# A tile of its own for a head's turned squares and spread root, in the second pass of a matrix memory

## The chip, the cores and the metric

The kernel runs on one core of one Trainium2 chip. The metric is device time in microseconds (us), taken as the median of several runs. Beside it stands one profiled execution, which tells when each instruction ran and what it waited for. The engines are named as in the profile: PE is the matmul engine (PEld its weight loads), DVE the vector engine, ACT the scalar engine, POOL the GpSimd engine, SP the engine that issues most DMAs.

## The reference

One encoder layer is applied to two inputs of 512 tokens by 1024 channels, `x_prompt` and `x_sample`, with the same weights: a half-step SwiGLU FFN, a mixing block, a second half-step FFN, a last RMSNorm. The mixing block runs grouped-query attention and an mLSTM matrix memory with 4 heads of 128 channels side by side. The change touches the end of the memory, where each head's output is normed over its 128 channels and gated:

```python
h = (h_fwd + h_bwd).transpose(0, 2, 1, 3)
h = h * lax.rsqrt(jnp.mean(h * h, axis=-1, keepdims=True) + EPS)
h = h.reshape(B, S, M_WIDTH) * head_norm.astype(jnp.float32)
return (jax.nn.sigmoid(o_pre.astype(jnp.float32)) * h).astype(q.dtype)
```

## The kernel before

All products are done in float32 split into a high and a low part (three matmuls for one product), on 128x512 tiles with channels on the partitions and the 512 tokens along the row. The mixing block is the generator `mix(s, ...)`, which runs once for each input; `s = 0` is the prompt, `s = 1` the sample. A scheduler orders the instructions of each engine by priority, and pools hand out tiles: a pool's tag has a fixed number of tiles, and a new tile of that tag starts when an older one's last user is done. Two tags matter here, both of 128x512 float32 tiles: `f2` with four tiles and `R` with two (`T2` at the top of the kernel hands them out, `F2()` in `mix` is `T2` with tag `f2`).

In the second pass (`s = 1`) the memory of a head goes through four steps, and the heads are interleaved with other products by the list at the end of `mix`'s memory part:

- `mem_head(h)` (L1291 and below) makes the weights of the head, four tiles of 128 tokens by 512. Its products on PE are L1302.
- `mem_blocks` turns them by DVE in 32x32 pieces into two tiles `qt` (L1340), and `mem_send` (L1348) lets POOL issue eight DMAs that write them to a DRAM buffer `tbuf`.
- `mem_out(h, ...)` fetches them back, turned as a whole: for each of the four blocks POOL issues a DMA into a tile `p = F2()` (L1361). In the profile this is `f<-tbuf`. Each block is split in two: ACT makes the upper half (L727) and DVE the lower half (L728, which also reads `p`, and so frees it). PE multiplies them with the values `Vm` (L1374, three matmuls for a block, twelve for a head). The marked instructions of this step keep their place in the program.
- Then the head is normed. ACT copies the result out of PSUM (L1380) and squares it (L1383). DVE turns the squares into `turned_` (L225, in `block_sums`), sums them to a small `row` (L226); PE folds `row` (L232); DVE makes the reciprocal root by small operations (L235 to L241), spreads it over `turned_` (L258, in `spread_rows`), and multiplies (L1391). ACT and DVE split the product into `mem` (L727, L728). The steps from L232 on carry a later priority, so they stand in the order behind work of the next head.

So `turned_` is written at L225, read at L226, written again at L258 and read last at L1391. It lives for about a head's time, while the next head's four blocks are being fetched into tiles of the same tag.

Beside this PE works through units of 24 or 12 matmuls (L850) that need no part of the memory: gates, and the projection of the attention (`merge_att`, `mg<-mg,mm` at L1269 on DVE). Their weights were split in the first pass and are loaded again by SP (L293, `w<-wpark`, two DMAs of 512 KB for a unit), into four tiles that come free when PE has finished a unit. SP also loads `w_out` (L271) into tiles that the sent `qt` tiles free. Near the end of the pass, `prep2` loads a tile of the first input from `x2buf` (L1808) into an `f2` tile, norms it on DVE (L723) and stores it to `xnbuf` (L1810). The `R` tiles hold rows that are spread over all partitions (`R2[0]`, which `prep2` reads) and running sums of squares.

Of the kernel before, what the change touches and what calls it, by code (L numbers as in the profile page):

```python
# [8 lines left out]
F32 = mybir.dt.float32  # L9
# [17 lines left out]
def encoder(ctx, tc, I, outs):  # L27
# [14 lines left out]
    def nm(s):  # L42
        n_id[0] += 1
        return f"{s}_{n_id[0]}"

    @contextmanager
    def shifted(n):

        tc.cur_priority += n
        yield  # L50
        tc.cur_priority -= n
# [8 lines left out]
    def T2(dtype=F32, tag="t2"):  # L60
        if tag in ("eb", "ac"):
            i = boxes[tag]
            boxes[tag] += 1
            return boxes["tile"][:, i % 4 + (4 if tag == "ac" else 0), :]
        if tag == "R":
            return spool.tile([P, S], dtype, tag="R", bufs=2, name=nm("R"))
        n = {"t2": 11, "f2": 4}[tag]
        return tpool.tile([P, S], dtype, tag=tag, bufs=n, name=nm(tag))
# [41 lines left out]
    def PO():  # L110
        return po_.tile([P, S], F32, tag="o", name=nm("pso"))
# [4 lines left out]
    def PT():  # L116
        return pt.tile([P, S], F32, tag="t", name=nm("pst"))
# [16 lines left out]
    def A(shape, dtype=F32, name="a"):  # L134
        return apool.tile(shape, dtype, tag="a", name=nm(name))
# [85 lines left out]
    def block_sums(t, q=None):  # L221

        row = spool.tile([P, 64], F32, tag="row", bufs=1, name=nm("row"))
        q = T2(F32, "f2") if q is None else q
        nc.vector.transpose(q, t)  # L225
        nc.vector.tensor_reduce(row[:, 0:16], q.rearrange("p (n j) -> p n j", j=32), axis=AX.X, op=ALU.add)  # L226
        return row

    def block_rstd(row, n, keep=lambda i: i):

        p = PT()
        keep(nc.tensor.matmul(p[:, 0:16], fold, row[:, 0:16], start=True, stop=True))  # L232
        V = nc.vector
        a, y, u = [row[:, 16 * i:16 * i + 16] for i in (1, 2, 3)]
        V.tensor_scalar(a, p[:, 0:16], 1.0 / n, EPS, op0=ALU.mult, op1=ALU.add)  # L235
        V.tensor_scalar(u.bitcast(I32), a.bitcast(I32), 1, None, op0=ALU.logical_shift_right)
        V.tensor_scalar(y.bitcast(I32), u.bitcast(I32), -1.0, 1597463007.0, op0=ALU.mult, op1=ALU.add)
        for _ in range(3):
            V.scalar_tensor_tensor(u, y, -0.5, y, op0=ALU.mult, op1=ALU.mult)
            V.tensor_tensor(u, u, a, op=ALU.mult)  # L240
            V.scalar_tensor_tensor(y, u, 1.5, y, op0=ALU.add, op1=ALU.mult)  # L241
        return y
# [13 lines left out]
    def spread_rows(r16, R):  # L256

        nc.vector.transpose(R.rearrange("p (n j) -> p n j", j=32), r16.unsqueeze(2).to_broadcast([P, 16, 32]))  # L258
        return R
# [465 lines left out]
    def split(src, hi, lo, eng=None):  # L725

        nc.scalar.activation(hi, src, AF.Copy)  # L727
        (eng or V_).tensor_tensor(lo, src, f(hi), op=ALU.subtract)  # L728
# [54 lines left out]
    def mark(i, last):  # L783
        return pin(i) if last and marks[0] else i
# [74 lines left out]
    def mix(s, xh, xl, early=None, extra=None, after=None):  # L859
# [9 lines left out]
        def F2(dtype=F32):  # L869
            return T2(dtype, "f2")  # L870
# [417 lines left out]
            return up_unit(1, d, mem, done, (PS, PT)[d % 2])  # L1288

        mem = A([P, HM, 2, S], F32R, "mem")  # L1290

        def mem_head(h):
            qk = qks[h]
# [58 lines left out]
        def mem_out(h, Ts):  # L1352
            moved = isinstance(Ts, int)
            vm = Vm[0]
            po = PO()
            hs_ = slice(h * P, (h + 1) * P)
            turned = []
            for j in range(4 + 1):
                if j < 4 and moved:
                    p = F2()  # L1360
                    mark(nc.gpsimd.dma_start(p, tbuf[Ts][4 * j:4 * j + 4].rearrange("c r a x -> (c r) (a x)")), True)  # L1361
                elif j < 4:
                    p = PT()
                    for i in range(4):
                        nc.tensor.transpose(p[:, i * P:(i + 1) * P], Ts[i][0][:, j * P:(j + 1) * P], ident)
                if j < 4:
                    ph, pl = T2(F32R), T2(F32R)
                    split(p, ph, pl)
                    turned.append((j, ph, pl))
                if j >= 1:  # L1370
                    t, ph, pl = turned.pop(0)
                    with shifted(15):
                        for n, (a, b) in enumerate(((0, ph), (1, ph), (0, pl))):
                            mark(nc.tensor.matmul(po, vm[:, a, t, hs_], b, start=(t == 0 and n == 0),  # L1374
                                                  stop=(t == 3 and n == 2)), True)
            h2 = T2()
            og = ogs[h]
            if moved:
                rows_ = T2()
                nc.scalar.activation(rows_.rearrange("p (i a m) -> p i a m", i=4, a=4),  # L1380
                                     po.rearrange("p (a i m) -> p i a m", i=4, a=4), AF.Copy)
                po = rows_
            nc.scalar.activation(h2, po, AF.Square)  # L1383
            V_.scalar_tensor_tensor(og, og, 1.0, po, op0=ALU.add, op1=ALU.mult)
            turned_ = F2()
            row = block_sums(h2, turned_)
            with shifted(60):
                rh = block_rstd(row, DM)
            with shifted(160):
                Rh = spread_rows(rh, turned_)  # L1390
                V_.scalar_tensor_tensor(og, og, hn[:, h:h + 1], Rh, op0=ALU.mult, op1=ALU.mult)  # L1391
                split(og, mem[:, h, 0, :], mem[:, h, 1, :])

        if s:
            qk2, qk3 = [[mem_qk(h, j) for j in range(2)] for h in (2, 3)]
            ma = [merge_att(d) for d in range(KD)]
            marks[0] = True
            q = mem_blocks(0, mem_head(0))
            at = [mem_send(*q)]
            go(*mem_values(), *qk2)  # L1400
            q = mem_blocks(1, mem_head(1))
            go(*qk3, ma[0], ma[1])
            mem_out(0, at[0])
            at.append(mem_send(*q))
            q = mem_blocks(2, mem_head(2))
            go(att_gate(6), att_gate(7), ma[2], ma[3])
            mem_out(1, at[1])
            at.append(mem_send(*q))
            q = mem_blocks(3, mem_head(3))
            go(*ma[4:])  # L1410
            mem_out(2, at[2])
            at.append(mem_send(*q))
            go(*[mem_gate(d) for d in range(EARLY)])
            mem_out(3, at[3])
            marks[0] = False
# [354 lines left out]
    R = [None, None]  # L1770
# [14 lines left out]
    def mid_parts(s):  # L1785
# [10 lines left out]
        return one, two, three  # L1796

    m0 = mix(0, *nhl[0], None, mid_parts(1), prep1)
    for _ in range(3):
        next(m0)  # L1800
# [27 lines left out]

    R2 = [None, None]
    m1 = mix(1, *nhl[1], None, parts2(0), prep2)  # L1830
    next(m1)
    next(m0)
# [150 lines left out]
```

## Time and profile before

| what | value |
|---|---|
| time, median of 3 runs | 2033.63 us (2033.22 to 2034.94) |
| profiled execution: time | 2034.22 us |
| profiled execution: span of the core | 2032.4 us |
| mean granted clock of PE over the span | 0.998 |
| busy: PE, DVE, ACT, POOL | 2016.1, 1593.8, 919.9, 253.4 us |
| second pass of the memory, from its first L1302 on PE to the start of its last L1391 | 1168.3 to 1311.9 us of the span |

The span runs from the first to the last instruction of the core; the time is longer by what lies around it. A row of the timeline gives start, length, engine, line and operation, the tiles written and read, how many instructions are merged in the row, and in brackets how long the engine stood idle before it and what released it. "Granted clock" is the share of PE's full clock that the chip allowed. Waits are inferred from semaphores: an instruction that waits for several is put down to the last of them.

### The profile page before, as it was taken

The numbers are of one execution on the slowest core, as the hardware profiler recorded it, in microseconds if no ns is written. First come the engines' busy times: TensorE is split into PE (matmuls) and PEld (weight loads), VectorE is DVE, ScalarE is ACT, GpSimd is POOL, SyncE is SP. The second block draws the span as 40 slices with busy tenths as digits, with TensorE's granted clock in tenths as the row PEclk, the third lists the DMA queues.
The fourth block names the chain that finished last, engine by engine and source line by source line (L and its number), as shares of the span: only waits on it lengthen the run. The fifth ranks groups of instructions, "written<-read, shape, count | busy, mean of one in ns | idle before, by whom it ended". The sixth has DMA issues, their size and how long they took to land.

```text
span 2032.4 us, 26876 instructions
## 1 busy us (share of the span) xinstructions
PE 2016.1 (99%) x9129; PEld 1662.1 (82%) x9129; DVE 1593.8 (78%) x2830; ACT 919.9 (45%) x1677; POOL 253.4 (12%) x313
## 2 busy tenths in 40 slices
PE   9999999999999999999999999999999999999998
PEld 7888888888888887888888877888888888888887
DVE  7989999996698787886567867367798988786797
ACT  7644444443224477663325754145444444442224
POOL 0233333301003000100120022011000000000001
PEclk9999999999999999999999999999999999999999
DMA  9778786899766765868556677767565655699753
GB/s 312 232 234 266 237 276 229 276 346 363 270 218 225 266 195 184 282 212 293 194 188 209 195 246 259 252 204 242 159 208 169 227 166 180 204 334 348 270 199 120
DMA packets 329546, 482.11 MB, mean 237 GB/s; under 512 B 23016, under 2 KB 196160, under 8 KB 328128
## 3 DMA queue, kind: packets, MB, share of 16 engines
q1 hardware_dynamic: 316352, 439.27, 64.9%
q0 software_dynamic: 12896, 40.86, 5.8%
q8 instruction: 72, 1.18, 0.2%
q14 instruction: 66, 0.54, 0.1%
q10 hardware_dynamic: 160, 0.27, 0.0%
HBM read 308.70 MB, written 171.61 MB: 236 GB/s over the span
## 4 chain that ended last, share of the span: by engine, by line
PE 94%; DVE 2%; DMA 2%; ACT 1%; issue 0%; SPq 0%; DVEq 0%; ACTq 0%; POOLq 0%
PE mm L850 15%; PE pso L374 12%; PE pst L374 11%; PE mm L374 10%; PE mm L644 9%; PE pss L374 6%; PE mm L836 4%; PE pss L644 4%; PE pst L644 4%; PE mm L815 3%; PE pso L644 3%; PE pss L1112 1%; PE pso L1159 1%; PE pst L850 1%; PE pss L850 1%; PE pss L1302 1%
## 5 line engine op out<-in xcount | busy, mean ns | idle before, releaser
L374 PE MATMUL pst<-xc,w 128*128 128x512 f32 x1056 | 253.8, 389 | 1.0 <-ACT t L409 1.0
L374 PEld LDWEIGHTS pst<-xc,w 128*128 128x128 f32 x1056 | 198.2, 188 | 42.5 <-ACT t L409 1.4
L374 PE MATMUL mm<-xc,w 128*128 128x512 f32 x972 | 229.7, 390 | 0.3 <-ACT f L382 0.3
L374 PEld LDWEIGHTS mm<-xc,w 128*128 128x128 f32 x972 | 181.9, 188 | 38.6 <-ACT f L382 0.8
L644 PE MATMUL mm<-rt,w 128*128 128x512 f32 x765 | 178.7, 389 | 0.0
L850 PE MATMUL mm<-xh,w 128*128 128x512 f32 x560 | 176.3, 392 | 0.0
L644 PEld LDWEIGHTS mm<-rt,w 128*128 128x128 f32 x765 | 143.5, 188 | 29.7
L332 ACT ACTIVATE w<-t 128x512 fp32r<-128x512 f32 x176 | 107.5, 628 | 132.2 <-issue 63.1
L333 DVE TENSOR_TENSOR w<-t,w 128x512 fp32r<-128x512 f32 x176 | 120.8, 704 | 30.6 <-ACT w L332 28.9
L374 PE MATMUL pso<-xc,f 128*128 128x512 f32 x528 | 127.2, 390 | 0.1
L374 PE MATMUL pss<-xc,w 128*128 128x512 f32 x528 | 126.8, 389 | 0.0
L374 PE MATMUL pso<-xc,w 128*128 128x512 f32 x528 | 126.8, 389 | 0.0
L850 PEld LDWEIGHTS mm<-xh,w 128*128 128x128 f32 x560 | 105.2, 188 | 22.0
L374 PEld LDWEIGHTS pso<-xc,f 128*128 128x128 f32 x528 | 98.9, 188 | 21.5 <-DVE t L413 1.0
L374 PEld LDWEIGHTS pss<-xc,w 128*128 128x128 f32 x528 | 99.1, 188 | 20.6
L374 PEld LDWEIGHTS pso<-xc,w 128*128 128x128 f32 x528 | 99.1, 188 | 20.6
L836 PE MATMUL mm<-xh,w 128*128 128x512 f32 x336 | 110.4, 395 | 0.0
L850 PE MATMUL mm<-xl,w 128*128 128x512 f32 x280 | 109.7, 392 | 0.0
L727 ACT ACTIVATE w<-wr 128x512 fp32r<-128x512 f32 x72 | 45.1, 632 | 138.4 <-PE pso L644 70.6
L727 ACT ACTIVATE w<-t 128x512 fp32r<-128x512 f32 x82 | 51.8, 632 | 107.4 <-PE pst L644 62.4
L644 PE MATMUL pss<-rt,w 128*128 128x512 f32 x396 | 93.7, 389 | 0.0
L644 PE MATMUL pst<-rt,w 128*128 128x512 f32 x396 | 93.7, 389 | 0.0
(461 smaller groups left out, 4169.6 us busy)
## 6 DMA issues: line engine op xcount, KB each, us to landing
rt<-rbuf SPq DMA_DIRECT2D x154, 512.0 KB, 5.7
w<-wpark SPq DMA_DIRECT2D x112, 512.0 KB, 5.0
wpark<-w SPq DMA_DIRECT2D x64, 512.0 KB, 3.9
wr<-in_ffn_w_gate_dram SPq DMA_DIRECT2D x62, 512.0 KB, 5.5
wr<-in_ffn_w_up_dram SPq DMA_DIRECT2D x44, 512.0 KB, 4.7
rbuf<-f SPq DMA_DIRECT2D x86, 256.0 KB, 4.5
rbuf<-R SPq DMA_DIRECT2D x82, 256.0 KB, 4.7
rbuf<-tab SPq DMA_DIRECT2D x74, 256.0 KB, 4.1
```

What stands on the lines that cost most here:

```text
L332: pin(nc.scalar.activation(t[:, 0], src, AF.Copy))
L333: pin(V_.tensor_tensor(t[:, 1], src, f(t[:, 0]), op=ALU.subtract))
L374: nc.tensor.matmul(p, a[:, k, :], xt[:, b, k, :], start=(first and k == 0 and i == 0), stop=(k == HK_ - 1 and i == 2), skip_group_check=True)
L644: nc.tensor.matmul(p, u[:, a, d * P:(d + 1) * P], r[:, b, ts], start=(first and q == 0 and k == 0), stop=(q == len(us) - 1 and k == 2), sk ...
L727: nc.scalar.activation(hi, src, AF.Copy)
L815: mark(nc.tensor.matmul(p[b][:, :N], a[:, k, bs], w_[:, kl, :], start=(k == 0 and i == 0), stop=(k == KD - 1 and i == 2)), (kl, b, i) == ( ...
L836: pin(nc.tensor.matmul(p[0], a[:, k, :], b, start=(k == 0 and i == 0), stop=(k == n - 1 and i == 2)))
L850: mark(nc.tensor.matmul(p, a[:, k, :], b, start=(k == 0 and i == 0), stop=last), last)
L1112: pin(nc.tensor.matmul(p, qT[:, h, b * P:(b + 1) * P], kv[:, hk * 2 + j, :], start=(j == 0), stop=(j == 1)))
L1159: pin(nc.tensor.matmul(pos[h], Vst[:, kb, h // 4, :], w, start=(kb == KBS[0] and i == 0), stop=(kb == KBS[3] and i == 1)))
L1302: nc.tensor.matmul(p, qk[a][:, isl], qk[b], start=(n == 0), stop=(n == 2))
```

## The change

```diff
@@ in mix(), after merge_mem, before mem_head
         mem = A([P, HM, 2, S], F32R, "mem")
+        own = [T2(F32, "R")] if s else []
 
@@ in mem_out()
             nc.scalar.activation(h2, po, AF.Square)
             V_.scalar_tensor_tensor(og, og, 1.0, po, op0=ALU.add, op1=ALU.mult)
-            turned_ = F2()
+            turned_ = own[0] if own else F2()
             row = block_sums(h2, turned_)
```

In the second pass, one tile of tag `R` is taken once, and all four heads use it as `turned_`. In the first pass nothing changes. No instruction is added or removed; lines behind the first edit move down by one (L1361 becomes L1362, L1374 becomes L1375, and so on). What moves is decided by the scheduler and the pools, and shows in the order at three places.

POOL, the fetches of head 2's four blocks and the sends of head 3, with the semaphores that each waits for (`DMASW` are POOL's own DMAs); before:

```order
L1361 DMA f_1450_11386<-tbuf_259 128x512 [waits DMASW2_49,DMASW1_49,DMASW3_49,DMASW0_49,DVE_49]
L1361 DMA f_1453_11392<-tbuf_259 128x512 [waits DVE_49]
L1361 DMA f_1456_11401<-tbuf_259 128x512 [waits DMASW6_49,DMASW5_49,DMASW7_49,DMASW4_49,DVE_49]
L1361 DMA f_1459_11410<-tbuf_259 128x512 [waits DMASW0_49,DVE_49,Activation_49]
L1348 DMA tbuf_260<-qt_11313 32x8x128 x4
```

and now:

```order
L1362 DMA f_1449_11385<-tbuf_259 128x512 [waits DMASW2_49,DMASW1_49,DMASW3_49,DMASW0_49,Activation_49]
L1362 DMA f_1452_11391<-tbuf_259 128x512 [waits DVE_49,Activation_49]
L1362 DMA f_1455_11400<-tbuf_259 128x512 [waits DMASW6_49,DMASW5_49,DMASW7_49,DMASW4_49,DVE_49]
L1362 DMA f_1458_11409<-tbuf_259 128x512 [waits DVE_49]
L1349 DMA tbuf_260<-qt_11312 32x8x128 [waits DVE_49]
```

The order is the same and the waits differ. Before, the fourth fetch needed the tile of head 2's own first block, and waited for its landing (`DMASW0`) and for ACT and DVE to split it. Now it waits for DVE alone, for the lower half of head 1's fourth block, which the third fetch of head 2 waited for before. The first send of head 3 now has a wait for its `qt` tile of its own.

DVE, from the first lower half of head 2 (L728 `t<-f,t`) to the sums of its squares; before:

```order
L728 TENSOR_TENSOR t_1452_11389<-f_1450_11386,t_1451_11388 128x512
L258 STREAM_TRANSPOSE f_1425_11212<-row_11213 128x512
L728 TENSOR_TENSOR t_1455_11395<-f_1453_11392,t_1454_11394 128x512
L1391 SCALAR_TENSOR_TENSOR box_5409<-box_5409,hn,f_1425_11212 128x512
L728 TENSOR_TENSOR t_1458_11404<-f_1456_11401,t_1457_11403 128x512
L728 TENSOR_TENSOR mem_10511<-box_5409,mem_10511 128x512
L1269 SCALAR_TENSOR_TENSOR mg_8644<-mg_8644,mm_11460 128x512
L728 TENSOR_TENSOR t_1461_11413<-f_1459_11410,t_1460_11412 128x512
L1384 SCALAR_TENSOR_TENSOR box_5409<-box_5409,t_1463_11423 128x512
L225 STREAM_TRANSPOSE f_1464_11427<-t_1462_11422 128x512
L1269 SCALAR_TENSOR_TENSOR mg_8644<-mg_8644,mm_11477 128x512
L226 TENSOR_REDUCE row_11428<-f_1464_11427 128x16
```

and now:

```order
L728 TENSOR_TENSOR t_1451_11388<-f_1449_11385,t_1450_11387 128x512
L258 STREAM_TRANSPOSE R_10512<-row_11212 128x512
L728 TENSOR_TENSOR t_1454_11394<-f_1452_11391,t_1453_11393 128x512
L1392 SCALAR_TENSOR_TENSOR box_5409<-box_5409,hn,R_10512 128x512
L728 TENSOR_TENSOR t_1457_11403<-f_1455_11400,t_1456_11402 128x512
L728 TENSOR_TENSOR t_1460_11412<-f_1458_11409,t_1459_11411 128x512
L728 TENSOR_TENSOR mem_10511<-box_5409,mem_10511 128x512
L1269 SCALAR_TENSOR_TENSOR mg_8644<-mg_8644,mm_11458 128x512
L1385 SCALAR_TENSOR_TENSOR box_5409<-box_5409,t_1462_11422 128x512
L225 STREAM_TRANSPOSE R_10512<-t_1461_11421 128x512
L226 TENSOR_REDUCE row_11426<-R_10512 128x16
L1269 SCALAR_TENSOR_TENSOR mg_8644<-mg_8644,mm_11475 128x512
```

The lower half of the fourth block moves up by two, ahead of `mem` and L1269, and L226 moves up by one.

PE, from the end of head 2's products (L1374, now L1375) to the fold of its `row` (L232); before:

```order
L1374 MATMUL pso_11385<-t_1457_11403,Vm_10719 128x512 x2
L850 MATMUL mm_11460<-att_9414,w_11354 128x512 x2
L1374 MATMUL pso_11385<-t_1458_11404,Vm_10719 128x512
L850 MATMUL mm_11477<-att_9414,w_11354 128x512 x3
L1374 MATMUL pso_11385<-t_1460_11412,Vm_10719 128x512 x2
L850 MATMUL mm_11477<-att_9414,w_11354 128x512 x3
L1374 MATMUL pso_11385<-t_1461_11413,Vm_10719 128x512
L850 MATMUL mm_11477<-att_9414,w_11354 128x512 x6
```

and now:

```order
L1375 MATMUL pso_11384<-t_1456_11402,Vm_10720 128x512 x2
L850 MATMUL mm_11458<-att_9414,w_11353 128x512 x2
L1375 MATMUL pso_11384<-t_1457_11403,Vm_10720 128x512
L1375 MATMUL pso_11384<-t_1459_11411,Vm_10720 128x512 x2
L1375 MATMUL pso_11384<-t_1460_11412,Vm_10720 128x512
L850 MATMUL mm_11475<-att_9414,w_11353 128x512 x12
```

The three matmuls of the fourth block stand up to six places earlier, directly behind those of the third. L232, nine matmuls further on before, moves up with them: from the last L1374 to L232 there were six L850 and nine more, and now there are twelve and three more.

On SP two things move: one load of `w_out` (L271) goes ahead of one pair of weight loads (L293), and at the end of the pass a fourth `x2buf` load and two of the `xnbuf` stores go ahead of another pair. ACT's and POOL's instructions stand in the order of before, but for two neighbours on ACT: the upper half of head 2's fourth block now goes ahead of the upper half of `mem`, and head 2's `mem` ahead of a gate (L884).

## The prediction

> **What bounds the kernel now.** I read the page's busy line first, then TensorE's own waits, then busy time in stretches of 50 us.
>
> ```profile
> span 2032.4 us, 26876 instructions
> ...
> PE 2016.1 (99%) x9129; PEld 1662.1 (82%) x9129; DVE 1593.8 (78%) x2830; ACT 919.9 (45%) x1677; POOL 253.4 (12%) x313
> ...
> PE pso L1374 <- ACT t L727: 2.5, 1, 2.5
> PE pst L1461 <- DVE xc L1546: 1.6, 1, 1.6
> ...
> PE pst L374 <- ACT t L409: 1.0, 1, 1.0
> ...
> 1250.00:1300.00 50.00, 47.48 (x202) 38.04 (x201) 26.75 (x83) 16.30 (x39) 7.90 (x14) 0.97 0.79 253
> 1300.00:1350.00 50.00, 50.00 (x223) 41.40 (x222) 34.28 (x61) 16.46 (x25) 0.00 (x0) 1.00 0.67 212
> 1800.00:1850.00 50.00, 48.98 (x217) 40.21 (x216) 34.68 (x56) 20.86 (x36) 0.00 (x0) 1.00 0.95 363
> ```
>
> The matmul engine (PE) is the bound: it is busy 99% of the span, so a change can gain only where PE waits, or where its clock falls. Its longest single wait, 2.5 us, is at L1374, the product of `mem_out`, and L1374 is next to the edited lines. The stretches (columns: length, busy time of PE, weight loads, DVE, ACT, POOL, then granted clock, DMA share, GB/s) say where: 1250 to 1300 has 202 matmuls and a clock of 0.97; the stretch after it has 223 and 1.00. The stretch 1800 to 1850, which also has about 1 us of idle PE, keeps a clock of 1.00.
>
> ```profile
> 1254.78 7.42 PE L850 MATMUL mm<-att,w 128*128 128x512 f32 x32
> 1262.03 0.61 PE L1374 MATMUL pso<-t,Vm 128*128 128x512 f32 x2
> ...
> 1266.61 0.45 PE L1374 MATMUL pso<-t,Vm 128*128 128x512 f32 x1
> 1266.89 0.86 PE L850 MATMUL mm<-att,w 128*128 128x512 f32 x3
> 1270.27 0.73 PE L1374 MATMUL pso<-t,Vm 128*128 128x512 f32 x2 [2.51 <-ACT t L727]
> ```
>
> In PE's timeline 32 matmuls start in 7.25 us (1254.78 to 1262.03), so one takes 0.2266 us. The three L850 from 1266.89 hold PE until 1267.57, and the next matmul starts at 1270.27: the stall costs **2.70 us** (the profile's 2.51 leaves out the modelled tail of the last matmul).
>
> ```profile
> 1270.30:1271.70 1.40, 1.40 (x6) 1.18 (x7) 0.64 (x1) 0.00 (x0) 0.26 (x2) 1.00 0.70 225
> 1271.70:1275.10 3.40, 3.40 (x9) 2.65 (x9) 1.88 (x3) 1.23 (x2) 1.52 (x3) 0.50 0.62 194
> 1275.10:1280.00 4.90, 4.90 (x24) 4.00 (x24) 3.25 (x15) 0.00 (x0) 0.00 (x0) 1.00 0.82 252
> ```
>
> Short stretches behind it show the clock at 0.50 for 3.40 us, then full again: **1.70 us** of work lost. No other 50 us stretch before the kernel's end is below 1.00, so I charge this dip to the stall. [...]
>
> Why PE waited is in the chain of waits:
>
> ```profile
> 1263.45 0.61 DVE t L728
> ...
> 1264.57 5.00 DMA f<-tbuf
> 1269.57 0.02 issue
> 1269.59 0.64 ACT t L727
> ```
>
> and in POOL's timeline:
>
> ```profile
> 1248.49 1.11 POOL L1361 DMA_DIRECT2D f<-tbuf  x2 [1.48 <-DMA tbuf<-qt]
> 1253.49 0.54 POOL L1361 DMA_DIRECT2D f<-tbuf  x1 [3.89 <-DVE row L239]
> 1264.57 0.54 POOL L1361 DMA_DIRECT2D f<-tbuf  x1 [10.53 <-DVE t L728]
> 1265.09 4.06 POOL L1348 DMA_DIRECT2D tbuf<-qt  x7
> ```
>
> Head 2's four gathered blocks come by four DMAs that POOL issues into the ring `f2` of four tiles. One tile of the four is held by head 1's `turned_`, which is still needed at L1391 (DVE, 1265.16). So three gathers go out by 1253.49, and the fourth waits 10.53 us until DVE has split block 0 and freed its tile; it lands 5.00 us after issue, and ACT, DVE and PE wait behind it.
>
> **The change part by part.** First, the tile. `turned_` moves out of `f2`, so four gathers fit. In the changed order the fourth gather of head 2 waits only for DVE's lower half of head 1's fourth block, which is the same wait that its third gather had before. The third was issued at 1253.49, so the fourth follows 0.54 later, at 1254.03. For its landing I take the 5.00 us of the row above: 1259.0. The view of the tile `f` has landings from 2.3 to 7.1 us, so 1256.3 to 1261.1 are the ends.
>
> ```profile
> 1259.54 1.14 ACT L727 ACTIVATE t<-f 128x512 fp32r<-128x512 f32 x2
> 1265.93 0.63 ACT L727 ACTIVATE mem<-box 128x512 fp32r<-128x512 f32 x1 [5.26 <-DVE box L1391]
> ...
> 1265.82 0.68 DVE L728 TENSOR_TENSOR t<-f,t 128x512 fp32r<-128x512 f32 x1
> 1266.60 0.69 DVE L728 TENSOR_TENSOR mem<-box,mem 128x512 fp32r<-128x512 f32 x1
> ...
> DMA to landing us min/median/max: 2.3/4.1/7.1
> ```
>
> ACT has nothing to do between 1260.68 and 1265.93, so the upper half of block 3 is ready by 1261.8 even at the late end. DVE now does the lower half right behind that of block 2 (1265.82): from 1266.45 to 1267.15. PE's order has the three matmuls of block 3 directly behind the one at 1266.61, the last at 1266.61 + 3 x 0.2266 = 1267.29. So the stall goes, with **0.14 us** to spare on DVE. If that cover is missing, PE waits for one DVE operation, 0.69 us at most by the nearest row (`mem`, 0.69); such a wait is below the 1.0 us that left the clock alone.
>
> Second, what is late next. The L232 product of head 2 moves nearer: 15 matmuls after the last L1374 as before, now all at full clock.
>
> ```profile
> 1271.54 0.46 PE L1374 MATMUL pso<-t,Vm 128*128 128x512 f32 x1
> ...
> 1272.09 0.60 ACT L1380 ACTIVATE t<-pso 128x512 f32<-128x512 f32 x1 [1.88 <-PE pso L1374]
> 1272.72 0.63 ACT L1383 ACTIVATE t<-t 128x512 f32<-128x512 f32 x1
> ...
> 1273.38 0.71 DVE L225 STREAM_TRANSPOSE f<-t 128x512 f32<-128x512 f32 x1
> ...
> 1275.20 0.68 DVE L226 TENSOR_REDUCE row<-f 128x16 f32<-128x512 f32 x1
> ```
>
> From the start of the last L1374 to that of L225 took 1.84 us; L225 needs 0.71 and L226, which now directly follows, 0.68: 3.2 us, so `row` is there at 1270.5. PE arrives at 1267.29 + 16 x 0.2266 = 1270.9. No wait, with 0.4 us of cover.
>
> Third, the operations themselves: the same transposes on a tile of the same size.
>
> ```profile
> L225 DVE STREAM_TRANSPOSE f<-t 128x512 f32<-128x512 f32 x4 | 2.8, 712 | 0.0
> ...
> L258 DVE STREAM_TRANSPOSE f<-row 128x512 f32<-128x512 f32 x4 | 2.8, 698 | 0.1
> ```
>
> No instruction is added and I cost them at nothing. The R ring has a tile that nobody uses in this stretch, so its first write waits for nothing.
>
> Fourth, the queues. POOL's eight sends of head 3 come out from under the late gather: 1265.09 becomes about 1262, when DVE has written their tiles. Nobody needs head 3's blocks before 1298, so that is worth nothing. On SP one `w_out` load moves ahead of a pair of weight loads, and at 1299 a fourth `x2buf` load and two `xnbuf` stores move ahead of another pair.
>
> ```profile
> 1262.22 13.16 SPq L293 DMA_DIRECT2D w<-wpark  x4
> ...
> w<-wpark SPq DMA_DIRECT2D x20, 512.0 KB, 5.4
> tbuf<-qt POOLq DMA_DIRECT2D x16, 128.0 KB, 4.3
> ```
>
> The `w_out` load waits for the first four sends of head 3, issued by 1264.3 (four at 4.06 / 7 = 0.58 us) and landed 4.3 us later, at 1268.6; the weight pair behind it waits for PE anyway, until 1270.0. A weight pair is used three units of 24 matmuls after its tile is freed, 16.3 us, and lands in 5.4 us, so 10.9 us of delay are hidden. I cost both edits at nothing.
>
> **The sum** is 2.70 + 1.70 = 4.40 us. The profiled execution took 2034.22 us, 1.82 around its span of 2032.4, so it becomes 2029.8. The median of the runs shown, 2033.63, is 0.59 lower, and the profiled time lies inside their range (2033.22 to 2034.94); from the median the sum is 2029.2. The verdict goes by medians, so I stay nearer to that: **2029.4 us**.
>
> **Rivals.** (1) Only the stall goes, 2.70 us. The dip begins 1.4 us after PE is back, so it hangs on some average over time, and where the stall falls in it may differ between executions: the runs that made the median may not have had it. For: the runs of before spread by 1.72 us, just the size of the dip. Against: one dip, right behind the one long stall. Time 2030.9 (from the median) to 2031.5. (2) A wait takes its place: DVE's margin of 0.14 us fails, or the gather lands late in a busy stretch. 0.69 us come back (2030.1), up to half of the stall with no dip (about 2030.8). (3) Nothing happens because the fourth gather is late for another reason, say the sends of head 2 that its third gather waited for: 2033.6 to 2034.2. Against: that third gather was out by 1253.49. (4) Slower: SP stands at the `w_out` load, and the weight pair behind it reaches PE late. It decides from 10.9 us of delay; to lose 0.2% beyond the gain it needs 10.9 + 4.4 + 4.1 = 19.4 us, against landings of at most 7.1. Time 2037.7 or more.
>
> **Chances.** Forecast 0.72, (1) 0.14, (2) 0.09, (3) 0.03, (4) 0.02. About 0.2%, 4.07 us here, is what a measurement of this kernel can tell from no change; that bound lies at 2029.56, inside the forecast's own spread of some 0.5 us. So two thirds of the forecast count as faster, and the rest of it with (1), (2) and (3) as the same: 0.48, 0.49 and 0.03. The range goes from 2028.4, the sum taken from the lowest run (2033.22 - 4.40 = 2028.8) with the same again for chance, to 2031.6, which takes in (1) and (2).
>
> **What would show it.** Right: POOL issues the fourth gather of head 2 within 1 us of the third; no wait of L1374 over 0.7 us; a clock of 1.00 in every stretch before the end; 1250 to 1300 with some 220 matmuls. Wrong: a new wait of PE on DVE at L1374 or L232, a wait on a weight DMA near 1290, or a dip that stays without the stall.

## The result, and the profile after

| | time, median | runs |
|---|---|---|
| before | 2034.76 us (2031.07 to 2037.59) | 22 |
| after | 2030.86 us (2028.89 to 2034.01) | 22 |

The ratio is 0.998, with a 95% interval of 0.9974 to 0.9986, so the change takes away 3.90 us (0.19%), with an interval of some 2.8 to 5.3 us. The profiled execution took 2029.29 us against 2034.22.

The page's head and TensorE's waits, longest first (what was waited for, us in total, times, longest), of the changed kernel:

```profile
span 2027.5 us, 26874 instructions
...
PE 2012.9 (99%) x9129; PEld 1660.2 (82%) x9129; DVE 1591.6 (79%) x2830; ACT 918.9 (45%) x1677; POOL 251.3 (12%) x313
...
PE pss L1303 <- DVE t L1319: 2.7, 3, 1.4
PE pst L1462 <- DVE xc L1547: 1.6, 1, 1.6
PE pst L374 <- ACT t L409: 0.8, 1, 0.8
```

The row `PE pso L1374`, 2.5 us, which led the list of before, has no successor at L1375. The others stood there before as well, and their lengths vary: the wait at about 1200 us (L1302, now L1303) was 0.58 and 0.71 us in two profiles of before, and 0.57 to 2.09 us in those of kernels with the changed ring. POOL's timeline and PE's timeline at head 2 show why:

```profile
1250.86 1.11 POOL L1362 DMA_DIRECT2D f<-tbuf  x2 [3.19 <-DVE row L226]
1253.97 1.07 POOL L1362 DMA_DIRECT2D f<-tbuf  x2 [1.99 <-DVE mg L1269]
1261.91 4.64 POOL L1349 DMA_DIRECT2D tbuf<-qt  x8 [6.87 <-DVE qt L1341]
```

```profile
1261.69 0.61 PE L1375 MATMUL pso<-t,Vm 128*128 128x512 f32 x2
...
1266.22 1.19 PE L1375 MATMUL pso<-t,Vm 128*128 128x512 f32 x4
1267.25 2.91 PE L850 MATMUL mm<-att,w 128*128 128x512 f32 x12
1270.01 0.39 PE L850 MATMUL mm<-xh,w 128*128 128x512 f32 x1
...
1270.69 0.29 PE L232 MATMUL pst<-row,fold 128*128 128x16 f32 x2
...
1293.39 0.73 PE L1375 MATMUL pso<-t,Vm 128*128 128x512 f32 x2
```

The third and the fourth gather now go out as one row of two at 1253.97, where the fourth stood 11.08 us behind the third. PE takes the last product of the third block and the three of the fourth as one row of four at 1266.22, without a wait ahead of them. The same stretch of 50 us, in the columns of before:

```profile
1250.00:1300.00 50.00, 50.00 (x222) 40.52 (x221) 29.61 (x87) 17.15 (x39) 9.00 (x16) 1.00 0.86 290
```

PE is busy in all of it, with 222 matmuls (202 before) and a clock of 1.00 (0.97 before).

The gain can be measured between two marks on PE that both kernels have: the first product of head 2 and the first product of head 3, with the same matmuls between. The second mark before is this row of PE's timeline:

```profile
1298.13 0.73 PE L1374 MATMUL pso<-t,Vm 128*128 128x512 f32 x2
```

Before, 1262.03 to 1298.13 is 36.10 us; after, 1261.69 to 1293.39 is 31.70 us. So **4.40 us** of the 4.9 us between the two spans come from this place, and the other 0.5 us lie ahead of it (0.34 us) and behind it. That is less than two profiles of one kernel differ by: the spans of the full change were 2027.5 us here and 2029.0 us in a later profile. A shorter pair of marks, from head 2's first product to the first `mm<-xh`, serves for the experiments: 12.33 us before (1262.03 to 1274.36), 8.32 us after (1261.69 to 1270.01). It leaves out the last 0.4 us that the dip costs.

### The profile page after: what moved, and what is told of

Its sections match the earlier page's. It is cut to its first block, busy times and chain, and to the rows that moved or that the text cites. A ratio compares the mean times of both kernels' runs of the same rounds, so it can differ in the third digit from the quotient of the medians.

```text
span 2027.5 us, 26874 instructions
## 1 busy us (share of the span) xinstructions
PE 2012.9 (99%) x9129; PEld 1660.2 (82%) x9129; DVE 1591.6 (79%) x2830; ACT 918.9 (45%) x1677; POOL 251.3 (12%) x313
## 4 chain that ended last, share of the span: by engine, by line
PE 94%; DVE 3%; DMA 1%; ACT 1%; issue 1%; SPq 0%; DVEq 0%; ACTq 0%
PE mm L850 16%; PE pst L374 11%; PE pso L374 11%; PE mm L374 11%; PE mm L644 9%; PE pss L374 6%; PE mm L836 4%; PE pst L644 4%; PE pss L644 4%; PE mm L815 3%; PE pso L644 3%; PE pss L1112 1%; PE pso L1159 1%; PE pso L1375 1%; PE pst L850 1%; PE pss L850 1%
## 5 line engine op out<-in xcount | busy, mean ns | idle before, releaser
L850 PE MATMUL mm<-xh,w 128*128 128x512 f32 x560 | 176.1, 391 | 0.0
L850 PEld LDWEIGHTS mm<-xh,w 128*128 128x128 f32 x560 | 104.9, 188 | 21.9
L850 PE MATMUL mm<-xl,w 128*128 128x512 f32 x280 | 109.6, 391 | 0.0
```

Source lines behind the costliest of these rows:

```text
L850: mark(nc.tensor.matmul(p, a[:, k, :], b, start=(k == 0 and i == 0), stop=last), last)
```

## The experiments

Below, "stretch" is that shorter pair of marks, and "wait" is PE's wait ahead of the last block of head 2's products.

### One head at a time

The tile of its own for head 1 alone, then for all heads but head 1, and the full change beside them on the same chip:

```diff
-            turned_ = own[0] if own else F2()
+            turned_ = own[0] if own and h == 1 else F2()
```

```diff
-            turned_ = own[0] if own else F2()
+            turned_ = own[0] if own and h != 1 else F2()
```

> Of the four heads of the second matrix memory only head 1 has its turned squares and spread root in the tile of their own; heads 0, 2 and 3 take a tile of the ring f2 as before. My theory (head 1's tile alone held back head 2's fourth gather): the whole gain stays. Head 2's fourth gather on GpSimd starts within 2 us of its third, TensorE has no wait of more than 0.7 us before the products of L1375 in head 2, the granted clock is 1.00 around 1270 us, and the time is that of the full change, 3 to 5 us under before. Rival (the gain is a sum over the heads, or comes from the ring being one tile freer everywhere): a quarter to a half of the gain, 1 to 2 us under before, with part of the wait left.

> The complement: heads 0, 2 and 3 have the tile of their own and head 1 alone takes a tile of the ring f2. My theory: nothing is gained. The fourth gather of head 2 starts some 11 us after the third, TensorE waits 2 to 3 us before the last block of head 2's products, a stretch of 3.4 us at clock 0.50 follows, and the time is within 0.7 us of before. Rival (the gain is a sum over heads): half or more of the gain, 2 us or more under before, with the fourth gather early.

> The full change once more, on the same chip as the two halves, to compare them with. Both theories: 3 to 5 us under before. If the 0.50 clock is not the stall's but comes in any execution at a moment of its own, a dip in the middle of the program shows in this profile too, at some place; by my theory there is none before the end.

| kernel | median (runs) | ratio to before (95%) |
|---|---|---|
| before | 2034.75 us (31) | |
| head 1 alone | 2031.09 us (11) | 0.9983 (0.9974 to 0.9992) |
| all but head 1 | 2034.96 us (11) | 1.0003 (0.9994 to 1.0012) |
| full change | 2030.72 us (11) | 0.9981 (0.9973 to 0.9990) |

POOL's timeline with head 1 alone:

```profile
1255.40 1.06 POOL L1362 DMA_DIRECT2D f<-tbuf  x2 [4.30 <-DMA tbuf<-qt]
```

and POOL's, then PE's, with all but head 1:

```profile
1255.37 0.54 POOL L1362 DMA_DIRECT2D f<-tbuf  x1 [3.97 <-DMA tbuf<-qt]
1266.11 0.54 POOL L1362 DMA_DIRECT2D f<-tbuf  x1 [10.20 <-DVE t L728]
```

```profile
1271.98 0.72 PE L1375 MATMUL pso<-t,Vm 128*128 128x512 f32 x2 [2.70 <-ACT t L727]
```

One tile in one head makes the whole difference. With head 1 alone the two gathers go out together, the wait is gone, the stretch is 8.28 us (1263.41 to 1271.69) and the median lies 3.66 us under before; with the other three heads the fourth gather is 10.74 us behind the third, the wait is 2.70 us, the clock is at 0.50 for 3.41 us from 1273.10 on, and the time is that of before. The profile of the full change shows no dip before the end of the program, as expected. The rival, a gain summed over the heads, falls: it wanted half or more of the gain from heads 0, 2 and 3, and the interval leaves them 1.2 us at most.

### The gather made late again, with the tile in place

If only the moment of the gather counts, it must be possible to undo the gain by delaying it and nothing else. Small copies on POOL stand between head 2's third and fourth gather of the full change; the order on PE, DVE and ACT is that of the full change.

```diff
                     p = F2()
+                    if h == 2 and j == 3:
+                        pad = small(4, "pad")
+                        for _ in range(27):
+                            mark(nc.gpsimd.tensor_copy(pad, hn), True)
```

The other kernels of the kind have 32, 46 and 54 for 27.

> The full change with 27 small copies (128x4; the kernel's own of that size took 186 ns each, so about 5.0 us) on GpSimd between head 2's third and fourth gather; every other engine's order is as in the full change. Theory (only the landing of that gather decides): in the changed kernel TensorE needs the fourth block 13.2 us after the third gather's start and a gather leads to TensorE's product 5.7 us after its own start (before: issue 1264.57, product 1270.27), so up to about 7 us of delay are free. No wait at L1375 over 0.7 us, clock 1.00, and 8.3 us from head 2's first product to the first of mm<-xh as in the full change. Rival (the early gather itself matters, through DMA or VectorE's order): the stretch grows by some us already here.

> As the kernels with 27, 46 and 54 copies, with 32: the copies came at some 0.28 us each there, not 0.186, so about 9.0 us of delay and the fourth gather some 9.5 us after the third. Theory: the wait before the last block is between the 0.58 us of 27 copies and the 2.70 us of before, about 1.5 us; that is less than half of a stretch of 3.41 us, so the clock stays 1.00 up to the end of the program. Rival (a wait of any length here brings a stretch at 0.50): a mean clock of 0.97 in 1250 to 1300 us.

> The same with 46 copies, about 8.6 us of delay. Theory: the fourth gather starts some 9.1 us after the third, TensorE's wait before the last block comes back at about 1.6 us (9.1 + 5.7 - 13.2), and the clock stays 1.00, because such a wait leaves TensorE busy for more than half of any 3.4 us: the stretch from the first product to mm<-xh is 9.9 us. Rival (any wait at this place brings the 0.50 clock): 1.3 to 1.7 us more in the stretch or behind it, and a mean clock of 0.97 in 1250 to 1300 us.

> The same with 54 copies, about 10.0 us of delay, which puts the gather where it stood before the change. Theory: the fourth gather starts some 10.6 us after the third, the wait is about 3.0 us, a stretch of 3.4 us at 0.50 follows, so that the whole of what the change gained is given back: 12 to 12.6 us from the first product to mm<-xh, and a mean clock of 0.97 in 1250 to 1300 us. Rival (the ring itself, not the gather's time, makes the difference): the stretch stays at 8.3 us.

One execution each, by its profile:

| copies | third gather to fourth | wait | at clock 0.50 | stretch |
|---|---|---|---|---|
| none (full change) | 0.5 us | none | none | 8.32 us |
| 27 | 7.85 us | 0.58 us | none | 9.42 us |
| 32 | 9.17 us | 3.69 us | 6.83 us | 14.78 us |
| 46 | 14.33 us | 4.71 us | 6.83 us | 15.14 us |
| 54 | 16.22 us | 6.72 us | 6.83 us | 17.66 us |

The rows of PE behind the wait, with 27 and with 32 copies:

```profile
1269.99 1.23 PE L1379 MATMUL pso<-t,Vm 128*128 128x512 f32 x3 [0.58 <-ACT t L727]
```

```profile
1270.23 1.65 PE L1379 MATMUL pso<-t,Vm 128*128 128x512 f32 x3 [3.69 <-ACT t L727]
```

The times of these single executions, 2032.37, 2035.63, 2040.41 and 2040.38 us, stand beside 2037.74 us for one run of before on the chip of 27, 46 and 54 copies, and a median of 2034.86 us on that of 32. Single runs spread too far to carry the argument, so the stretch is read.

The gain goes with the gather: 7.85 us of lateness cost 1.1 us of the stretch, and 9.17 us bring back more than the change had gained there. The rival that the ring itself makes the difference falls, since the ring is the changed one in all four. The sizes were off in two ways. A copy took 0.186 to 0.188 us in the median, as expected, but some took longer (up to 0.40 us among the 27, up to 0.72 us among the 46), and there was idle time between them (1.6 us among the 27), so they came every 0.27 to 0.30 us. All delays are longer than meant, and the wait of about 1.5 us that 32 or 46 copies were to make was never made: what such a wait does to the clock is not shown by them, and the half of 3.4 us in both expectations was the author's estimate. With 27 copies the stretch was expected at the full change's 8.3 us and came out at 9.42. And the gather's own duration is not one number. These are the issues of the fourth gather, with size and time from issue to landing, in the full change (where the row holds the third as well), with 32 copies, and with 46:

```profile
f<-tbuf POOLq DMA_DIRECT2D x2, 256.0 KB, 2.9
```

```profile
w<-wpark SPq DMA_DIRECT2D x1, 512.0 KB, 7.2
f<-tbuf POOLq DMA_DIRECT2D x1, 256.0 KB, 7.1
```

```profile
f<-tbuf POOLq DMA_DIRECT2D x1, 256.0 KB, 2.9
```

With 32 copies the gather is issued at 1262.36, 0.66 us behind two weight loads of 512 KB:

```profile
1261.70 0.82 SPq L293 DMA_DIRECT2D w<-wpark  x2
```

It lands after 7.1 us; with 46 copies it is issued 5.9 us behind that pair (1266.27 and 1272.17) and takes 2.9 us. The gather of before went out 2.35 us behind the pair (1262.22 and 1264.57) and took 5.0 us. The busy rows of the four flights, in the full change, with 46 copies, in the kernel before and with 32 copies (the DMA share is the last number but one):

```profile
1254.50:1257.40 2.90, 2.90 (x15) 2.39 (x14) 2.76 (x19) 0.99 (x4) 0.54 (x2) 1.00 0.58 184
```

```profile
1272.17:1275.07 2.90, 0.00 (x0) 0.00 (x0) 0.00 (x0) 0.00 (x0) 2.90 (x6) 0.64 0.44 143
```

```profile
1264.57:1269.57 5.00, 3.19 (x14) 2.13 (x12) 3.22 (x6) 0.63 (x1) 4.58 (x8) 1.00 1.05 379
```

```profile
1262.36:1269.46 7.10, 4.19 (x18) 3.01 (x17) 3.63 (x6) 0.00 (x0) 4.60 (x8) 0.96 1.08 356
```

The two short flights found the DMA engines half free (0.58 and 0.44), the two long ones found them full (1.05 and 1.08). The other profiles fit: where the gather waits for the ring (all but head 1, the filled wait, before once more) it went out 2.34 or 2.35 us behind a pair and took 5.2 to 5.4 us; with 27 copies it went out 0.59 us ahead of a pair and took 5.3 us; with 54 copies it went out 7.86 us behind one and took 2.9 us. POOL's sends follow the gather in all the late cases, also in the two that took 2.9 us. So the lateness was paid twice in the kernel before: it also put the gather behind a pair of weight loads. This is read from where the loads stood; no run moves them alone.

### The wait filled with work

In the kernel before, ten extra products into a spare PSUM tile stand ahead of the last block, so that PE works through most of the wait. The gather stays late. Three products of `mm<-att` that stood ahead of the wait come behind it in this kernel's order. The extra products are read by nobody.

```diff
+                    if h == 2 and t == 3 and moved:
+                        spare = PT()
+                        for _ in range(10):
+                            mark(nc.tensor.matmul(spare, vm[:, 0, 2, hs_], last_ph, start=True, stop=True), True)
+                    last_ph = ph
                     with shifted(15):
```

> The kernel before with 10 extra products of 128x512 into a spare PSUM tile on TensorE, ahead of the last block of head 2's products, so that TensorE works through most of the 2.70 us it waits there (10 x 0.23 = 2.3 us, of which 0.69 take the place of three products of mm<-att that now come later). The gather stays late. Theory (the 0.50 clock is the idle time's): the idle time left is about 1.1 us, the clock stays 1.00 and the first mm<-xh comes 3.5 us after the wait's end, against 4.09 us in the profile of before (1270.27 to 1274.36). Rival (the dip comes from the work behind the wait or at a moment of its own): a stretch of 3.4 us at 0.50 follows all the same, with 4.5 us or more to the first mm<-xh.

PE's timeline, and busy time from the wait's end to the first `mm<-xh` (the columns are those of the 50 us stretches):

```profile
1267.35 2.45 PE L1375 MATMUL pst<-t,Vm 128*128 128x512 f32 x10
1270.90 1.22 PE L1379 MATMUL pso<-t,Vm 128*128 128x512 f32 x3 [1.11 <-ACT t L727]
1271.96 2.91 PE L850 MATMUL mm<-att,w 128*128 128x512 f32 x12
1274.71 0.39 PE L850 MATMUL mm<-xh,w 128*128 128x512 f32 x1
```

```profile
1250.00:1300.00 50.00, 48.89 (x214) 39.09 (x213) 27.29 (x83) 16.84 (x40) 9.02 (x16) 1.00 0.80 260
1270.90:1274.71 3.81, 3.81 (x15) 2.85 (x16) 2.50 (x4) 1.23 (x2) 1.81 (x4) 1.00 0.57 156
```

The gather is as late as before (10.70 us behind the third), 1.11 us of the wait are left, and the clock stays 1.00. Fifteen matmuls take 3.81 us behind the wait (3.5 us were expected), where before twelve took 4.09 us and the dip had 0.4 us still to cost. So the dip hangs on PE's idle time, and not on the late gather, on the work behind it, or on a moment of its own.

### The kernel before, once more

> The kernel before, once more. Both theories: a wait of 2.7 us (2.5 to 2.9) before the last block of head 2's products. Theory: the clock is set from stretches of 3.41 us one after another, whose beginning has nothing to do with the program; one that held 1.97 us of the wait was followed by a stretch at 0.50 in the profile of before, and one that held 1.75 us (with 54 copies) was not. A boundary that falls between 0.8 and 1.9 us into the wait cuts it into two parts that are both too short, so in about 3 of 10 executions the dip is missing; where it comes, it starts between 0.9 us before the wait's end and 1.6 us after it. Rival (the dip follows every such wait by a fixed delay): a dip here too, 1.1 to 1.5 us behind the wait's end; and if the clock dips at a moment of its own, it comes at another place.

PE's timeline:

```profile
1272.37 0.74 PE L1374 MATMUL pso<-t,Vm 128*128 128x512 f32 x2 [2.95 <-ACT t L727]
```

In the first profile of before the record of the clock begins at 8.78 us, at full, falls to 0.50 at 1271.71, is full again at 1275.12 and falls at 2029.47: 370, 371 and 592 times 3.413 us after its beginning. In the profile of the changed kernel it begins at 6.18 us, at full, and falls at 2023.46, 591 times 3.413 us later. PE's first matmul starts at 1.63 us in both, so where these steps lie in the program differs between the two executions. Busy time in pieces of 3.41 us that begin or end where the clock changes, for the first profile of before, this execution of it, with 54 copies, and with 46 (PE's busy time is the first number behind the comma, and the clock stands third from the end):

```profile
1268.29:1271.71 3.42, 1.44 (x6) 1.22 (x7) 0.69 (x1) 0.63 (x1) 1.59 (x4) 1.00 0.88 298
1271.71:1275.12 3.41, 3.41 (x9) 2.65 (x9) 1.90 (x3) 1.23 (x2) 1.51 (x3) 0.50 0.63 196
1275.12:1278.53 3.41, 3.41 (x17) 2.79 (x16) 1.96 (x9) 0.00 (x0) 0.00 (x0) 1.00 0.77 215
```

```profile
1269.54:1272.96 3.42, 0.59 (x3) 0.51 (x4) 0.63 (x2) 0.63 (x1) 1.88 (x4) 1.00 0.83 286
1272.96:1276.37 3.41, 3.41 (x10) 2.63 (x9) 0.91 (x3) 1.23 (x2) 1.66 (x3) 0.50 0.58 155
1276.37:1279.78 3.41, 3.41 (x17) 2.84 (x16) 2.34 (x6) 0.00 (x0) 0.00 (x0) 1.00 0.66 181
```

```profile
1267.51:1270.93 3.42, 1.82 (x8) 1.11 (x6) 1.26 (x2) 0.00 (x0) 2.75 (x12) 1.00 0.70 272
1270.93:1274.34 3.41, 0.00 (x0) 0.00 (x0) 0.00 (x0) 0.00 (x0) 3.06 (x10) 1.00 0.20 26
1274.34:1277.75 3.41, 1.70 (x4) 1.38 (x5) 1.72 (x3) 1.15 (x2) 3.20 (x6) 0.50 0.88 260
1277.75:1281.17 3.42, 3.42 (x9) 2.68 (x9) 2.23 (x4) 1.23 (x2) 1.73 (x4) 0.50 0.79 224
```

```profile
1269.57:1272.98 3.41, 1.56 (x7) 0.88 (x5) 1.00 (x2) 0.00 (x0) 2.93 (x10) 1.00 0.57 228
1272.98:1276.39 3.41, 0.55 (x1) 0.50 (x2) 0.57 (x1) 1.15 (x2) 3.41 (x7) 0.50 0.74 208
```

In these rows the clock of a piece goes with PE's busy share in the piece before it, and not with its own: behind a share of 53% (1.82 of 3.42, with 54 copies) the clock was full though PE stood through the whole piece, and behind 46% (1.56 of 3.41, with 46 copies), 42% (1.44 of 3.42, the first profile of before) and 17% (0.59 of 3.42, here) it was 0.50. In the first profile of before, cut so from end to end, all pieces at full clock but the one with 42% and the one ahead of the fall at 2029.47, in which PE stood, had 70% or more; in that of the changed kernel the lowest piece that kept the full clock had 60% (2.04 of 3.41, from 1197.43), and the one ahead of the fall at 2023.46 had 19% (0.65 of 3.42). At 46% both were seen: with both memories on four tiles (the last experiment), a piece near the end of the program was followed by one at full clock.

```profile
2016.02:2019.43 3.41, 1.58 (x14) 1.37 (x12) 3.07 (x10) 2.69 (x9) 0.00 (x0) 1.00 0.53 195
2019.43:2022.85 3.42, 0.00 (x0) 0.00 (x0) 0.78 (x2) 0.72 (x1) 0.00 (x0) 1.00 0.83 310
```

What happens between 46% and 53% these rows do not show, and the shares are rough, since the profile models PE's busy time. The longest wait with no dip behind it was 2.1 us, in the second profile of the full change. The rival of a fixed delay falls: the dip began 1.44 us behind the wait's end in the first profile of before, 0.59 us here, and with 46 and 54 copies while PE still stood. That the dip can be missing where a border cuts the wait was not seen: all three profiles with a wait of 2.5 to 2.95 us have it. Every run has a mean granted clock on record, to three digits. On the chip of the one-head experiments it averages 0.9985 over the 42 runs of the kernels with the wait (before, and all but head 1) and 0.9990 over the 22 of those without it (head 1 alone, and the full change). One dip in every run would make a difference of 0.0008 (1.70 of 2033 us); the difference is 0.0006, so most of the runs had the dip, and whether all had it stays open.

### A third and fourth PSUM tile for the scores

The largest sum of PE's waits left in the changed kernel, 2.7 us, is that of the scores (L1303) for DVE to have read the block two before. The second memory needs the two tiles `pst` at that time only for the fold of `row` (L232), so the blocks can take turns on them; then the same in both memories.

```diff
-                p = PS()
+                p = (PS, PT)[i % 2]() if s else PS()
```

```diff
-                p = PS()
+                p = (PS, PT)[i % 2]()
```

> On top of the full change, the second matrix memory's scores (L1302 on, four blocks of rows a head) alternate between the PSUM tiles pss and pst instead of pss alone, so that a block need not wait for VectorE to have read the one two before it. In the profile of the changed kernel the second of the blocks at 1200.74 us waits 1.36 us for VectorE's L1319. Theory: this wait goes and nothing comes in its place, 1 to 1.4 us under the full change (about 5 us under before). Rival: VectorE and ScalarE, which make what the next blocks and heads need, set that place, so the wait moves by some us and comes back elsewhere, or the pst tiles are late for the spread root: within 0.5 us of the full change, or slower by up to 1 us.

> The scores of the second matrix memory alone on pss and pst, once more, beside the kernel with both. Its median was 1.97 us under the full change's, with intervals that overlap; the wait that it takes away was 1.36 to 2.1 us in two profiles of the full change. Theory: the gain over before is 5 to 6.5 us again, a ratio of 0.9968 to 0.9976. Rival (the difference was chance): 0.998 or above.

> On top of the full change, the scores' blocks alternate between pss and pst in both matrix memories, the first and the second; in the first one pst also takes the transposed blocks. The profile with pst in the second alone still has two waits of TensorE at these scores in the first, 1.6 us together. Theory: they go too, 1 to 1.6 us under the kernel with pst in the second alone. Rival (in the first memory the transposed blocks need pst, and now wait for it): same time as that kernel within 0.7 us, or slower by 1 to 3 us, with new waits at L1366.

| kernel | median (runs) | before beside it | ratio to before (95%) |
|---|---|---|---|
| second memory, first time | 2028.75 us (9) | 2034.75 us | 0.9973 (0.9963 to 0.9982) |
| second memory, again | 2029.14 us (8) | 2034.86 us | 0.9971 (0.9960 to 0.9981) |
| both memories | 2027.46 us (5) | 2034.86 us | 0.9965 (0.9953 to 0.9978) |

PE's waits with both memories on four tiles:

```profile
PE pst L1462 <- DVE xc L1547: 1.6, 1, 1.6
...
PE pst L1366 <- DVE t L1331: 0.5, 1, 0.5
```

No wait at L1303 is left, and the transposed blocks of the first memory, which share `pst`, wait for 0.5 us that they did not wait before. Twice the second memory's edit came out under the full change's ratio (0.9973 and 0.9971 against 0.9981); the first time it lay 1.97 us under the full change, where 1 to 1.4 us were expected. Once the edit in both came out lowest, 7.40 us under before and 1.68 us under the second memory alone. The intervals of these kernels overlap, so that each is faster than before is shown; that they beat the full change is likely and not settled.

## Why the prediction was right, point by point

- **The cause.** "One tile of the four is held by head 1's `turned_`": shown by head 1 alone, which keeps the gain, and by the other three heads, which keep the wait. With it the third rival, another reason for the late gather, falls.
- **The sum, 2.70 + 1.70 = 4.40 us.** Between the two marks on PE 4.40 us went. That this meets the sum to the hundredth is luck: the same marks lie 36.25 us apart with all heads but head 1 and 36.52 us in the second profile of before, and 31.67 and 31.66 us with head 1 alone and in the second profile of the full change, so other pairs of profiles give up to 4.9 us. The medians differ by 3.90 us, and by 4.03 us in the second comparison; 4.40 us lies inside both intervals. The predicted level, 2029.4 us, was worked out from a median of before of 2033.63 us from three runs; the comparison's median of before is 2034.76 us from 22, which accounts for 1.1 of the 1.5 us by which the forecast lies below 2030.86.
- **The dip is the stall's.** Filling the stall took the dip away with the gather as late as ever. That speaks against the first rival, and so does the mean granted clock of the runs, which is lower where the wait is. The medians alone decide less: a gain of 2.70 us lies just outside the first interval (2.8 to 5.3 us) and inside that of the second comparison (2.0 to 5.5 us), and the time that the first rival named, 2030.9 us, is the one that was measured, because the median of before came out 1.1 us above the one it started from. The piece of 3.41 us ahead of the dip was not idle throughout: PE was busy for 42% of it in the first profile of before, and with 54 copies the full clock stayed behind a piece with 53%.
- **The fourth gather** was forecast 0.54 us behind the third, and the two make one row of 1.07 us. Its landing is the term that was mis-sized: I took the 5.00 us of the late gather, while the early one, which found the DMA engines at a share of 0.58, took 2.9 us. It did not matter, since the block was then waited for by DVE's order and not by the DMA; with 27 copies, 7.85 us of lateness and a flight of 5.3 us still made a wait of only 0.58 us.
- **DVE's margin of 0.14 us** held. The rows of the changed kernel have the two lower halves, the last at 1265.48 + 1.28 = 1266.76, and PE's three products of that block go without a gap until 1267.25. The last of them, which reads the lower half, starts at about 1266.90 (1266.22 and three times 0.2266), again 0.14 us later:

```profile
1264.82 0.74 DVE L1392 SCALAR_TENSOR_TENSOR box<-box,hn,R 128x512 f32<-128x512 f32 x1
1265.48 1.28 DVE L728 TENSOR_TENSOR t<-f,t 128x512 fp32r<-128x512 f32 x2
...
1269.55 0.69 DVE L226 TENSOR_REDUCE row<-R 128x16 f32<-128x512 f32 x1
```

- **L232** was forecast at 1270.9 with `row` ready at 1270.5; it came at 1270.69, with `row` ready at 1270.24. The second rival, a wait that takes the stall's place, did not come.
- **The queues.** Head 3's sends were forecast at about 1262 and went out at 1261.91. No wait of PE on a weight DMA stands in the list of waits, so the price of nothing for SP's moved loads holds, and with it the fourth rival falls.

## What to carry to other kernels

A tile that lives long in a ring of short-lived ones takes one tile from every other user of the ring: look for the one transfer that is issued late although its queue is idle, follow its wait back to the tile, and give the long-lived tile a place of its own. Price a stall of the matmul engine with the clock behind it, and read that clock in short stretches: here 2.70 us of waiting cost 4.40 us, with 3.41 us at 0.50 behind it, and a wait of 1.1 us cost no clock. When a transfer is moved in time, take its duration from what else is on the DMA engines at the new time, not from where it stood: here 5.00 us were taken, and 2.9 us came.

## What the runs showed of the hardware

- In the first profile of before the clock changed 370, 371 and 592 times 3.413 us after the beginning of its record, in that of the changed kernel 591 times.
- Behind a piece of 3.41 us with PE's busy share at 60% (the changed kernel, from 1197.43) and 53% (54 copies, from 1267.51) the clock was full, at 42% (before, from 1268.29) and 17% (before once more, from 1269.54) it was 0.50, and at 46% it was 0.50 once (46 copies, from 1269.57) and full once (both memories on four tiles, from 2016.02). Behind a piece at 0.50 it was full again where PE was busy throughout (before, from 1271.71) and 0.50 again with a share of 50% (54 copies, from 1274.34). Since busy time is modelled, these shares are rough.
- The same 256 KB gather took 2.9, 5.0 or 7.1 us with the DMA engines' share at 0.58, 1.05 and 1.08 during its flight, the last two 2.35 and 0.66 us behind a pair of 512 KB weight loads.
- A chain of copies of 128x4 on POOL into one tile came at 0.27 to 0.30 us a copy, though the median copy took 0.186 to 0.188 us; four of the kernel's own of that size, into different places, took 0.55 us together (L977, before, from 662.14).
